# Rounded products first: reordering the products of transposed blocks in an attention kernel

## The chip, the cores and the metric

The kernel runs on one core of one Trainium2 chip, as one launch. The metric is device time in microseconds (us). TensorE is called PE in the rows (its weight loads PEld), VectorE is DVE, ScalarE is ACT, GpSimd is POOL and SyncE, which issues the transfers, is SP.

## The reference

One inference step of a one-layer encoder for two request groups, a prompt of 1024 rows and a sample of 64 rows with a cache of 1024 past rows, with shared weights:

```
shift/scale/gate (x2) = silu(c) @ w_ada + b_ada                      # adaLN, one column set per group
h   = RMSNorm(x) * (1 + scale1) + shift1
u   = h @ w_in                                                       # 1024 -> 3072
mix = concat(differential attention (4 heads), stick-breaking attention (8 heads))
x   = x + gate1 * RMSNorm(mix @ w_out)
x   = x + gate2 * RMSNorm(relu(h2 @ w_up)^2 @ w_down),  h2 as h, with shift2, scale2
```

All data are float32. A differential head applies `softmax(q0 k0) - lam * softmax(q1 k1)` to its values; a stick-breaking head weighs key k by `sigmoid(z_k)` times the product of `1 - sigmoid(z)` over the later keys. Both end in a matrix of weights, queries by keys, times the values.

## The kernel before, in words

**Rounded part and remainder.** Matrix products run in a rounded float32 format. To keep precision, an operand is split: ACT casts it to the rounded format (line 64), and DVE (for some, POOL) subtracts the cast from the original (line 65), which leaves the remainder. A product is then the sum of two or three products into one accumulator. Names that end in h are rounded parts, those that end in l remainders.

**Attention.** Work is cut into units u = 0 to 7: units 0 to 3 are one differential head each, units 4 to 7 are two stick-breaking heads each. A unit has steps: `Diff(u, t)` for 128 query rows, `Stick(u, q, hd)` for 256 query rows of one head, `Sample(u)` for the sample group. A step has a score part (lines 593 and 594 make `pz`; ACT takes exponentials or sigmoids, and a stick-breaking head runs a DVE scan, line 740) and an apply part. The apply part works in groups of up to four 128x128 blocks: PE transposes the blocks into `pt` (line 604), ACT casts `pt` to `ah` (line 64), DVE subtracts to `al` (line 65), and PE multiplies both with the values into `po`. A group is named by its step, as in `ah6_110`: unit 6, q = 1, head 1, blocks 0; `ahS60` is the sample step of unit 6, first cache half.

In `apply_rows` (for Diff and Sample, lines 616 to 623) the blocks are the stationary operand: block by block, a product of 256 columns with `ah` (line 620), then one of 128 columns with `al` (line 621). In `Stick.apply` (lines 781 to 789) the values are stationary and `ah` or `al` streams: for each of two key blocks j, a product with `ah` (line 788), then one with `al` (line 789), 256 columns each, or 128 for the block on the diagonal. `ah` and `al` have two buffers each.

**adaLN's second columns.** `modulation` (line 212) makes shift2 and scale2 in eight pieces during attention: products into `pam` (line 201), a DVE copy to `Rm` (line 224), a small product with `sel` into `pcm` (line 209), then DVE additions.

**What sets the order.** The text interleaves one step's apply with the next step's score (`merge`), and spends a filler between them: projections of the next unit (lines 303 to 305), and from unit 2 on the pieces of `modulation` and `gate_rows`. A generator's `yield c` says how much estimated PE time it has spent; the filler stops at a yield when its debt is paid. On top of this, the program is built with `schedule_with_timeline_sim=True` (line 1302): at build time the framework lays out each engine's list from its own estimate of when each instruction will be ready, and takes first what stands first in the text. So work of other steps stands between neighbours of the text, and a change in the text moves instructions on all engines. On the chip each engine follows its list strictly; a wait stops all that stands behind it there.

**After attention** come the output projection (`py`, lines 1095 to 1098), whose first products are laid between the last attention steps, and the feed-forward part (`pu`, lines 303 to 305; `pd`, lines 1181 to 1184).

Of the kernel before, what the change touches and what calls it, by code (L numbers as in the profile page):

```python
# [16 lines left out]
P = 128  # L17
# [17 lines left out]
def build(tc, I, O):  # L35
# [11 lines left out]
    def big(name, tag, shape, dt=F32R):  # L47
        return sb.tile(shape, dt, tag=tag, name=name, bufs=BUFS[tag])
# [4 lines left out]
    def brief(shape, name, tag, dt=F32, bufs=2):  # L53
        return atp.tile(shape, dt, tag=tag, name=name, bufs=bufs)

    def bank(name, tag):
        return pp.tile([P, 512], F32, tag=tag, name=name)

    load = nc.sync.dma_start
    mm = nc.tensor.matmul  # L60
# [60 lines left out]
    cc = brief([16, P], "cc", "o1", bufs=1)  # L121
# [66 lines left out]
    def ada_rows(c0, name, ps=None, between=()):  # L188


        if ps is None:
            ps = bank("pa" + name, "pj")[:, :256]
        for q in range(2):
            raw = ada_raws.get((c0, q))
            if raw is None:
                raw = big(f"ar{name}{q}", "raw", [P, 4, 256], F32)
                load(raw, w_ada[:, 4 * q : 4 * q + 4, c0 : c0 + 256])
            if q == 1 and between:
                between.pop()()
            for i in range(4):  # L200
                mm(ps[32 * i : 32 * i + 32], lhsT=sc[:, 4 * q + i, :], rhs=raw[:, i, :], start=(q == 0), stop=(q == 1), skip_group_check=True)
            yield 0.5
        return ps

    def sum_to_columns(R, n, name):

        ps = bank(name, "pj")
        for i in range(n):
            mm(ps[:, 2 * i : 2 * i + 2], lhsT=R[:, i * P : (i + 1) * P], rhs=sel, start=True, stop=True)
        return ps[:, 0 : 2 * n].rearrange("p (k j) -> p k j", j=2)  # L210

    def modulation(first, cols, name):

        A, B = (sb.tile([P, KT, 2], F32, name=x + name) for x in "AB")

        def gen():
            for q in range(4):
                ks = slice(2 * q, 2 * q + 2)
                for part in range(2):
                    nm = f"{name}{q}{part}"  # L220
                    c0 = first + D * part + 256 * q
                    ps = yield from ada_rows(c0, nm)
                    R = big("R" + nm, "s", [P, 512], F32)[:, :256]
                    nc.vector.tensor_copy(R, ps)
                    v = sum_to_columns(R, 2, "pc" + nm)
                    col = lambda c: cols[:, c : c + 2].unsqueeze(2).broadcast_to([P, 2, 2])
                    o = (B, A)[part][:, ks, :]
                    nc.vector.tensor_tensor(o, v, col(8 + (c0 - first) // P), ALU.add)
                    if part:
                        nc.vector.scalar_tensor_tensor(o, o, 1.0, col(2 * q), ALU.add, ALU.mult)  # L230
                    yield None

        return A, B, gen()
# [366 lines left out]
    def transposed(srcs, name, kr=P):  # L600

        pt = bank("pt" + name, "tr")
        for i, a in enumerate(srcs):
            nc.tensor.transpose(pt[:kr, i * P : (i + 1) * P], a, ident)  # L604
        n = len(srcs) * P
        ah, al = (small([P, 512], f"{x}{name}", x, F32R, bufs=2) for x in ("ah", "al"))
        split(pt[:kr, :n], ah[:kr, :n], al[:kr, :n])
        return ah, al

    def apply_rows(po, parts, values):  # L610

        n = sum(len(p[0]) for p in parts)
        done = 0
        pend = []

        def times(ah, al, blocks, kr):
            nonlocal done
            for i in range(len(blocks)):
                v = values(done)
                mm(po[:, 0:256], lhsT=ah[:kr, i * P : (i + 1) * P], rhs=v.rearrange("p a d -> p (a d)"), start=(done == 0), stop=False, skip_group_check=True)  # L620
                mm(po[:, 0:P], lhsT=al[:kr, i * P : (i + 1) * P], rhs=v[:, 0, :], start=False, stop=(done == n - 1), skip_group_check=True)
                done += 1

        for blocks, kr, name, pre in parts:
            if pre:
                pre()
            pend.append((*transposed(blocks, name, kr), blocks, kr))
            yield 0.11 * len(blocks)
            if len(pend) == 2:
                times(*pend.pop(0))  # L630
                yield 0.8
        yield 0.1
        while pend:
            times(*pend.pop(0))
            yield 0.8
# [17 lines left out]
    class Diff:  # L653
# [37 lines left out]
        def apply(self):  # L691
            u, t = self.u, self.t
            V = U[u]["V"]
            self.po = po = bank(f"po{self.name}", "pv")
            parts = []
            for c, (c0, w) in enumerate(chunks(P * (t + 1))):
                e0, e1 = self.e[0][c], self.e[1][c]

                def pre(e0=e0, e1=e1):
                    nc.vector.scalar_tensor_tensor(e0, e1, self.cf, e0, ALU.mult, ALU.add)  # L700

                parts.append(([e0[:, i : i + P] for i in range(0, w, P)], P, f"{self.name}{c}", pre))
            yield from apply_rows(po, parts, lambda j: V[:, j])
            le = brief([P, 1], f"le{self.name}", "le", bufs=1)
            nc.gpsimd.tensor_scalar(le, self.l[0], self.l[0], EPS, ALU.mult, ALU.mult)
            od = brief([P, P], f"od{self.name}", "od", bufs=1)
            o1 = brief([P, P], f"o1{self.name}", "o1", bufs=1)
            nc.scalar.copy(o1, po[:, P:256])
            nc.vector.tensor_tensor(od, po[:, 0:P], o1, ALU.add)
            r = rstd(sumsq([od], P, f"ssd{self.name}", [o1]), P, f"rsd{self.name}", add=le, inv=1.0 / P)  # L710
            nc.gpsimd.tensor_scalar(od, od, r, None, ALU.mult)
            self.od = od
# [34 lines left out]
    class Stick:  # L747
# [26 lines left out]
        def apply(self):  # L774
            u, q, hd = self.u, self.q, self.hd
            r, o = slice(64 * hd, 64 * hd + 64), slice(64 - 64 * hd, 128 - 64 * hd)
            V = U[u]["V"]
            po = bank(f"po{self.name}", "pv")
            pend = []

            def times(jp, ah, al):
                for i in range(2):
                    j = 2 * jp + i
                    v = V[:, j, hd, :]
                    lone = j == 2 * q + 1
                    out = po[:, P:256] if lone else po[:, 0:256]
                    cc = slice(256, 384) if lone else slice(256 * i, 256 * i + 256)
                    mm(out, lhsT=v, rhs=ah[:, cc], start=(j == 2 * q), stop=False, skip_group_check=True)  # L788
                    mm(out, lhsT=v, rhs=al[:, cc], start=False, stop=(j == 1), skip_group_check=True)  # L789

            for jp in reversed(range(q + 1)):
                blocks = [(j, t) for j in (2 * jp, 2 * jp + 1) for t in range(2) if not (j == 2 * q + 1 and t == 0)]
                src = [self.w[t][j // 4][:, (j % 4) * P : (j % 4 + 1) * P] for j, t in blocks]
                pend.append((jp, *transposed(src, f"{self.name}{jp}")))
                yield 0.11 * len(src)
                if len(pend) == 2:
                    times(*pend.pop(0))
                    yield 0.43
            yield 0.1
            while pend:  # L800
                times(*pend.pop(0))
                yield 0.43
            if hd == 0:
                mixes[u] = brief([P, 256], f"mx{self.name}", "mx", bufs=1)
            mx = mixes[u]
            ot = brief([P, 256], f"ot{self.name}", "so2", bufs=1)
            nc.scalar.copy(ot[r], po[o, 0:256])
            nc.vector.tensor_tensor(mx[r], po[r, 0:256], ot[r], ALU.add)
            if hd == 1:
                load(mixD[u, :, 256 * q : 256 * q + 256], mx)  # L810
# [421 lines left out]
    for b in range(NB - 1):  # L1232
# [12 lines left out]
        if last:  # L1245
            GG2 = gate("g2", 1, "h")
            wd2 = [down_weights(b + 1, i, i == 0) for i in range(2)]
            done = []
# [57 lines left out]
```

## Time and profile before

| | us |
|---|---|
| three runs | 1546.62, 1553.53, 1556.1 (median 1553.53) |
| profiled execution | 1554.56 |
| its span, first to last instruction | 1552.7 |
| PE busy in the span | 1499.0 (97%), 8714 products and as many weight loads |
| DVE, ACT, POOL busy | 918.1 (59%), 700.1 (45%), 342.7 (22%) |
| mean granted TensorE clock | 0.99 |

Attention lies between about 60 and 690 us of the span, the output projection runs to about 780 us, and the feed-forward part from there to the end. A row of the timeline gives start, duration, engine, line, operation, output<-inputs, and shapes; a bracket at its end is the idle time of the engine ahead of it and what ended it. Starts of PE's products are closer together than their durations, since one product streams in while the one ahead drains; the pace is the distance of the starts. The granted clock is 1.00 at 2.4 GHz and 0.5 at 1.2 GHz.

### The profile page before, as it was taken

The numbers are of one execution on the slowest core, as the hardware profiler recorded it, in microseconds if no ns is written. First come the engines' busy times: TensorE is split into PE (matmuls) and PEld (weight loads), VectorE is DVE, ScalarE is ACT, GpSimd is POOL, SyncE is SP. The second block draws the span as 40 slices with busy tenths as digits, with TensorE's granted clock in tenths as the row PEclk, the third lists the DMA queues.
The fourth block names the chain that finished last, engine by engine and source line by source line (L and its number), as shares of the span: only waits on it lengthen the run. The fifth ranks groups of instructions, "written<-read, shape, count | busy, mean of one in ns | idle before, by whom it ended". The sixth has DMA issues, their size and how long they took to land.

```text
span 1552.7 us, 23586 instructions
## 1 busy us (share of the span) xinstructions
PE 1499.0 (97%) x8714; PEld 1341.8 (86%) x8714; DVE 918.1 (59%) x1761; ACT 700.1 (45%) x1650; POOL 342.7 (22%) x519
## 2 busy tenths in 40 slices
PE   6899999989999999899999999999999999999998
PEld 4789898878899988778898988899989999899896
DVE  3776877675868687866442445454554544544447
ACT  3766766666768577837653112121122112121122
POOL 1453443434333333622110000000000000000002
PEclk9999999999999999999999999999999999999999
DMA  9322333424232325444221122211111111111025
GB/s 315 119 60 82 93 115 100 119 62 124 71 113 60 111 88 159 124 122 140 75 66 52 34 79 82 70 40 41 55 54 41 46 37 42 54 55 41 28 82 183
DMA packets 152517, 133.20 MB, mean 86 GB/s; under 512 B 11234, under 2 KB 136275, under 8 KB 152403
## 3 DMA queue, kind: packets, MB, share of 16 engines
q1 hardware_dynamic: 152402, 131.71, 27.6%
q8 instruction: 68, 1.11, 0.3%
q14 instruction: 47, 0.38, 0.1%
HBM read 108.59 MB, written 23.09 MB: 85 GB/s over the span
## 4 chain that ended last, share of the span: by engine, by line
PE 64%; issue 4%; ACT 4%; DVE 3%; POOL 1%; DMA 1%; SPq 0%; DVEq 0%; POOLq 0%; ACTq 0%
PE pu L303 8%; PE pu L305 8%; PE pu L304 8%; PE pd L1181 8%; PE pd L1182 8%; PE pd L1184 7%; PE py L1096 1%; PE py L1098 1%; PE pt L604 1%; PE py L1095 1%; PE po L789 1%; PE pq L303 1%; PE pq L305 1%; PE pq L304 1%; PE pk L303 1%
## 5 line engine op out<-in xcount | busy, mean ns | idle before, releaser
L1188 DVE TENSOR_TENSOR acc<-pd,acc 128x512 f32<-128x512 f32 x252 | 171.8, 687 | 113.6 <-PE pd L1184 107.8
L1166 ACT ACTIVATE sq<-pu 128x384 f32<-128x384 f32 (+1 forms) x96 | 45.1, 470 | 308.3 <-PE pu L305 308.3
L1167 DVE TENSOR_TENSOR sq<-sq 128x384 f32<-128x384 f32 (+1 forms) x96 | 72.1, 751 | 171.8 <-ACT sq L1166 171.8
L65 DVE TENSOR_TENSOR al<-pt,ah 128x512 fp32r<-128x512 f32 (+2 forms) x128 | 75.6, 598 | 19.1 <-ACT ah L64 17.7
L593 PE MATMUL pz<-K,Q 128*128 128x128 f32 (+2 forms) x192 | 72.9, 382 | 4.5 <-DVE mn L678 1.9
L64 ACT CAST ah<-pt 128x512 fp32r<-128x512 f32 (+2 forms) x128 | 65.9, 522 | 24.5 <-PE pt L604 16.7
L604 PE MATMUL pt<-ident,s 128*128 128x128 f32 x432 | 70.0, 277 | 4.2 <-DVE al L65 1.5
L642 ACT ACTIVATE s<-s,mn 128x512 f32<-128x512 f32 (+3 forms) x96 | 58.6, 611 | 23.3 <-DVE mn L678 19.7
L594 PE MATMUL pz<-Kl,qz 128*128 128x128 f32 (+2 forms) x192 | 66.6, 350 | 0.0
L740 DVE TENSOR_TENSOR_SCAN s<-k,s 128x128 f32<-128x128 f32 (+1 forms) x64 | 58.2, 922 | 11.4 <-POOL s L769 7.1
L604 PEld LDWEIGHTS pt<-ident,s 128*128 128x128 f32 x432 | 51.6, 141 | 9.2 <-DVE al L65 2.0
L65 DVE TENSOR_TENSOR rl<-sq,rh 128x384 fp32r<-128x384 f32 x64 | 35.7, 558 | 38.1 <-ACT rh L64 38.1
L442 POOL CAST qz<-Q 64x256 fp32r<-64x256 f32 x64 | 36.9, 576 | 90.5 <-PE pz L594 71.8
L764 ACT ACTIVATE s<-pz 128x128 f32<-128x128 f32 (+2 forms) x96 | 47.8, 498 | 15.5 <-PE pz L594 14.9
L64 ACT CAST rh<-sq 128x384 fp32r<-128x384 f32 x64 | 32.8, 513 | 40.2 <-DVE sq L1167 38.2
L765 ACT ACTIVATE k<-pz 128x128 f32<-128x128 f32 (+2 forms) x96 | 47.9, 499 | 0.0
L789 PE MATMUL po<-al,V 128*128 128x256 f32 (+1 forms) x160 | 41.4, 293 | 6.3 <-DVE al L65 6.3
L740 DVE TENSOR_TENSOR_SCAN s<-k,s,s 128x512 f32<-128x512 f32 x32 | 43.6, 1371 | 5.1 <-ACT k L765 5.1
L593 PEld LDWEIGHTS pz<-K,Q 128*128 128x128 f32 x192 | 36.6, 191 | 11.2 <-DVE mn L678 4.6
L678 DVE CUSTOM_DVE_ANT_0 s<-pz,T 128x512 f32<-128x512 f32 (+3 forms) x64 | 37.3, 585 | 12.4 <-PE pz L594 11.9
L788 PE MATMUL po<-ah,V 128*128 128x256 f32 (+1 forms) x160 | 43.8, 284 | 0.7 <-ACT ah L64 0.7
L64 ACT CAST r<-sq 128x320 fp32r<-128x320 f32 x32 | 14.8, 461 | 62.7 <-DVE sq L1167 62.7
(1232 smaller groups left out, 5125.5 us busy)
## 6 DMA issues: line engine op xcount, KB each, us to landing
arr<-in_w_ada SPq DMA_DIRECT2D x16, 512.0 KB
arm<-in_w_ada SPq DMA_DIRECT2D x16, 512.0 KB
ar<-in_w_ada SPq DMA_DIRECT2D x10, 512.0 KB
mixD<-mx SPq DMA_DIRECT2D x32, 128.0 KB
xr<-in_x_prompt SPq DMA_DIRECT2D x16, 256.0 KB
xD<-xr SPq DMA_DIRECT2D x16, 256.0 KB
xy<-xD SPq DMA_DIRECT2D x8, 512.0 KB
out_y_prompt<-xy SPq DMA_DIRECT2D x16, 256.0 KB
```

Source lines behind the costliest of these rows:

```text
L64: (eh or nc.scalar.copy)(hi, src)
L65: (el or nc.vector).tensor_tensor(lo, src, fr(hi), ALU.subtract)
L303: mm(ps[:, :n], lhsT=wh[:, k, :], rhs=hh[:, k, :n], start=(k == 0), stop=False)
L304: mm(ps[:, :n], lhsT=wh[:, k, :], rhs=hl[:, k, :n], start=False, stop=False)
L305: mm(ps[:, :n], lhsT=wl[:, k, :], rhs=hh[:, k, :n], start=False, stop=(k == 7))
L593: mm(ps[:, :w], lhsT=S["Q"][m][:, qt], rhs=S["Kd"][m][:, c0 : c0 + w], start=True, stop=False)
L604: nc.tensor.transpose(pt[:kr, i * P : (i + 1) * P], a, ident)
L740: nc.vector.tensor_tensor_scan(d, k, d, 0.0 if later is None else later[:, 0:1], ALU.mult, ALU.add)
L1181: mm(ps, lhsT=rh[:, off : off + P], rhs=wh[:, cols], start=(j == 0), stop=False)
L1182: mm(ps, lhsT=rh[:, off : off + P], rhs=wl[:, cols], start=False, stop=(m == 8 and end))
L1184: mm(ps, lhsT=rl[:, off : off + P], rhs=wh[:, cols], start=False, stop=end)
L1188: nc.vector.tensor_tensor(acc[m][:, cols], ps, acc[m][:, cols], ALU.add)
```

## The change

Three places of the text. In `apply_rows` and in `Stick.apply` the products of a group with the rounded parts come first for all its blocks, then those with the remainders. In `modulation` a yield of 0.2 stands after the copy to `Rm`, so that the filler may stop there and other work may be laid ahead of the product with `sel`. No instruction is added or taken away on any engine.

```diff
@@ modulation
                     R = big("R" + nm, "s", [P, 512], F32)[:, :256]
                     nc.vector.tensor_copy(R, ps)
+                    yield 0.2
                     v = sum_to_columns(R, 2, "pc" + nm)
@@ apply_rows
         def times(ah, al, blocks, kr):
             nonlocal done
-            for i in range(len(blocks)):
-                v = values(done)
-                mm(po[:, 0:256], lhsT=ah[:kr, i * P : (i + 1) * P], rhs=v.rearrange("p a d -> p (a d)"), start=(done == 0), stop=False, skip_group_check=True)
-                mm(po[:, 0:P], lhsT=al[:kr, i * P : (i + 1) * P], rhs=v[:, 0, :], start=False, stop=(done == n - 1), skip_group_check=True)
-                done += 1
+            vs = [values(done + i) for i in range(len(blocks))]
+            for i, v in enumerate(vs):
+                mm(po[:, 0:256], lhsT=ah[:kr, i * P : (i + 1) * P], rhs=v.rearrange("p a d -> p (a d)"), start=(done + i == 0), stop=False, skip_group_check=True)
+            for i, v in enumerate(vs):
+                mm(po[:, 0:P], lhsT=al[:kr, i * P : (i + 1) * P], rhs=v[:, 0, :], start=False, stop=(done + i == n - 1), skip_group_check=True)
+            done += len(blocks)
@@ Stick.apply
             def times(jp, ah, al):
-                for i in range(2):
-                    j = 2 * jp + i
-                    v = V[:, j, hd, :]
-                    lone = j == 2 * q + 1
-                    out = po[:, P:256] if lone else po[:, 0:256]
-                    cc = slice(256, 384) if lone else slice(256 * i, 256 * i + 256)
-                    mm(out, lhsT=v, rhs=ah[:, cc], start=(j == 2 * q), stop=False, skip_group_check=True)
-                    mm(out, lhsT=v, rhs=al[:, cc], start=False, stop=(j == 1), skip_group_check=True)
+                for a in (ah, al):
+                    for j in (2 * jp, 2 * jp + 1):
+                        lone = j == 2 * q + 1
+                        out = po[:, P:256] if lone else po[:, 0:256]
+                        c0 = 256 * (j % 2)
+                        mm(out, lhsT=V[:, j, hd, :], rhs=a[:, c0 : c0 + (P if lone else 256)], start=(a is ah and j == 2 * q),
+                           stop=(a is al and j == 1), skip_group_check=True)
```

What it moves is more than these lines show. Three places follow, each before and then with the change; line numbers grow by one with the change, and by two behind `apply_rows`' first lines.

**On PE, at the end of unit 6's sample step** (`poS6`, with `ahS61` and `alS61` of its second cache half, `ahS60` and `alS60` of its first; `pv72` is a projection for unit 7). Before:

```order
L620 MATMUL poS6_8267<-cv61_8143,ahS61_8291 128x256
L621 MATMUL poS6_8267<-cv61_8143,alS61_8292 128x128
L604 MATMUL pt7_101_8364<-ident_66,s7_1020_8255 128x128
L604 MATMUL pt7_101_8364<-ident_66,s7_1030_8274 128x128 x2
L620 MATMUL poS6_8267<-cv60_8142,ahS60_8316 128x256
L593 MATMUL pz7_2041_8439<-K70_7606,Q70_7501 128x128
L594 MATMUL pz7_2041_8439<-Kl7_7608,qz0_493 128x128
L593 MATMUL pz7_2051_8457<-K70_7606,Q70_7501 128x256
L594 MATMUL pz7_2051_8457<-Kl7_7608,qz0_493 128x256
L621 MATMUL poS6_8267<-cv60_8142,alS60_8317 128x128
```

With the change, where "..." stands for 20 more products into `pv72`:

```order
L621 MATMUL poS6_8284<-cv61_8156,ahS61_8305 128x256 x4
L304 MATMUL pv72_8414<-h1h2_119,wv7h_7496 128x320
L305 MATMUL pv72_8414<-h1l2_120,wv7h_7496 128x320
...
L304 MATMUL pv72_8414<-h1h2_119,wv7h_7496 128x320
L594 MATMUL pz7_2041_8445<-K70_7606,Q70_7501 128x128
L595 MATMUL pz7_2041_8445<-Kl7_7608,qz0_493 128x128
L623 MATMUL poS6_8284<-cv61_8156,alS61_8306 128x128 x4
L621 MATMUL poS6_8284<-cv60_8155,ahS60_8322 128x256 x4
L623 MATMUL poS6_8284<-cv60_8155,alS60_8323 128x128 x4
L605 MATMUL pt7_101_8370<-ident_66,s7_1020_8272 128x128
L605 MATMUL pt7_101_8370<-ident_66,s7_1030_8291 128x128 x2
```

Before, S61's remainder follows each of its rounded products at once, and four score products (`pz7`) stand between the first product with `ahS60` and the first with `alS60`; now 22 projection and two score products stand between S61's four rounded products and its remainders, S60's follow behind, and the transposes of group 7_101 come behind all of it instead of ahead.

**On DVE, over the same stretch** (the scans of line 740 are printed as SCALAR_TENSOR_TENSOR here and write `s7_...`, `ml1` is a remainder for the output projection, `Kl7` one of unit 7's keys). Before:

```order
L65 TENSOR_TENSOR alS61_8292<-ptS61_8286,ahS61_8291 128x512
L740 SCALAR_TENSOR_TENSOR s7_1030_8274<-k7_1030_8275,s7_1030_8274 128x512
L65 TENSOR_TENSOR ml1_9029<-ml1_9029,mh1_9028 128x1152
L489 SCALAR_TENSOR_TENSOR Q71_7502<-pq72_8222,Q71_7502 64x256
L65 TENSOR_TENSOR alS60_8317<-ptS60_8311,ahS60_8316 128x512
L740 SCALAR_TENSOR_TENSOR s7_1120_8351<-k7_1120_8352,s7_1120_8351 128x384
L514 TENSOR_TENSOR Kl7_7608<-pk72_8304,K70_7606 64x256
L740 SCALAR_TENSOR_TENSOR s7_1130_8372<-k7_1130_8373,s7_1130_8372 128x512
L65 TENSOR_TENSOR al7_101_8369<-pt7_101_8364,ah7_101_8368 128x384
```

With the change:

```order
L65 TENSOR_TENSOR alS61_8306<-ptS61_8300,ahS61_8305 128x512
L65 TENSOR_TENSOR alS60_8323<-ptS60_8317,ahS60_8322 128x512
L742 SCALAR_TENSOR_TENSOR s7_1030_8291<-k7_1030_8292,s7_1030_8291 128x512
L742 SCALAR_TENSOR_TENSOR s7_1120_8357<-k7_1120_8358,s7_1120_8357 128x384
L515 TENSOR_TENSOR Kl7_7608<-pk72_8267,K70_7606 64x256
L515 TENSOR_TENSOR Kl7_7608<-pk72_8267,K71_7607 64x256
L742 SCALAR_TENSOR_TENSOR s7_1130_8378<-k7_1130_8379,s7_1130_8378 128x512
L742 SCALAR_TENSOR_TENSOR s7_2041_8443<-k7_2041_8444,s7_2041_8443 128x128
L932 TENSOR_TENSOR sod6_8352<-so26_8351 64x64 x2
L465 COPY ok72_8400<-pnk72_8396 128x256
L468 COPY ok72_8400<-pnk72_8396 64x128
L65 TENSOR_TENSOR al7_101_8375<-pt7_101_8370,ah7_101_8374 128x384
```

The subtraction for S60 moved ahead of the scan `s7_1030`, from four places behind S61's to the next one; the subtraction for 7_101 moved back, behind `Kl7`, a scan and copies.

**On PE, group 6_110 of unit 6** (`pt6_110` are its transposes; `pq70` is a projection). Before, where the first "..." stands for three more products of group 6_111, five transposes, two score products and 15 products into `pq70`, the second for two more into `pq70`, two score products and three transposes:

```order
L604 MATMUL pt6_110_7440<-ident_66,s6_1130_7333 128x128
L593 MATMUL pz6_2141_7524<-K61_6556,Q61_6455 128x128
L594 MATMUL pz6_2141_7524<-Kl6_6557,qz1_494 128x128
L788 MATMUL po6_11_7416<-ah6_111_7421,V6_6667 128x256
...
L788 MATMUL po6_11_7416<-ah6_110_7445,V6_6667 128x256
...
L789 MATMUL po6_11_7416<-al6_110_7446,V6_6667 128x256
L788 MATMUL po6_11_7416<-ah6_110_7445,V6_6667 128x256
L789 MATMUL po6_11_7416<-al6_110_7446,V6_6667 128x256
```

With the change:

```order
L605 MATMUL pt6_110_7434<-ident_66,s6_1130_7327 128x128
L594 MATMUL pz6_2050_7466<-K60_6559,Q60_6468 128x512
...
L789 MATMUL po6_11_7413<-ah6_111_7418,V6_6667 128x256
L789 MATMUL po6_11_7413<-ah6_111_7418,V6_6667 128x128
L789 MATMUL po6_11_7413<-al6_111_7419,V6_6667 128x256
L789 MATMUL po6_11_7413<-al6_111_7419,V6_6667 128x128
...
L605 MATMUL pt6_202_7529<-ident_66,s6_2051_7422 128x128 x2
L594 MATMUL pz6_2141_7521<-K61_6560,Q61_6469 128x128
L595 MATMUL pz6_2141_7521<-Kl6_6561,qz1_494 128x128
L789 MATMUL po6_11_7413<-ah6_110_7439,V6_6667 128x256 x2
...
L789 MATMUL po6_11_7413<-al6_110_7440,V6_6667 128x256 x2
```

Left out here are a score product, a transpose and two transposes of values. The 17 projection products that stood between the transposes of 6_110 and its remainders are gone from there, so its products follow its transposes much sooner. Between the last product into `pam` of the eight pieces of adaLN's columns and the first into `pcm` there stand, piece by piece, 1, 3, 14, 14, 18, 13, 14 and 7 instructions of other steps before, and 8, 7, 17, 15, 25, 13, 17 and 1 with the change. Of the output projection, 19 products of `py11` stand ahead of the product with `alS72` (unit 7's sample step) before, and behind it with the change.

## Rows read from the trace of the kernel before

**Rows 1.** The page, busy time by engine: us, share of the span, instructions.

```profile
PE 1499.0 (97%) x8714; PEld 1341.8 (86%) x8714; DVE 918.1 (59%) x1761; ACT 700.1 (45%) x1650; POOL 342.7 (22%) x519
```

**Rows 2.** Stages: length; busy us by engine; granted clock, DMA share, GB/s.

```profile
80.00:600.00 520.00, 503.68 (x3409) 464.04 (x3408) 375.59 (x882) 354.29 (x942) 200.93 (x320) 1.00 0.31 92
600.00:690.00 90.00, 79.65 (x473) 68.32 (x472) 70.67 (x99) 59.65 (x128) 46.54 (x47) 0.94 0.47 145
780.00:1553.00 773.00, 765.51 (x4022) 688.85 (x4021) 378.91 (x587) 181.84 (x327) 51.98 (x48) 1.00 0.19 59
```

**Rows 3.** PE's waits, 60 to 740 us: total us, times, longest.

```profile
PE po L789 <- DVE al L65: 6.3, 9, 1.1
PE poS L621 <- DVE alS L65: 3.8, 2, 2.2
PE pcm L209 <- DVE Rm L224: 3.1, 4, 1.0
```

**Rows 4.** Timeline of PE: the pace of products with fresh weights.

```profile
245.51 0.33 PE L620 MATMUL po<-V,ah 128*128 128x256 f32 x1
245.68 0.22 PE L621 MATMUL po<-V,al 128*128 128x128 f32 x1
245.74 0.44 PE L594 MATMUL pz<-Kl,qz 128*128 128x512 f32 x1
...
654.99 0.28 PE L867 MATMUL pzS<-Kn,bd 128*128 128x64 f32 x1
655.10 0.28 PE L868 MATMUL pzS<-Kn,bd 128*128 128x64 f32 x1
...
655.87 0.28 PE L789 MATMUL po<-al,V 128*128 128x256 f32 x1
655.99 0.28 PE L788 MATMUL po<-ah,V 128*128 128x256 f32 x1
```

**Rows 5.** Timeline of PE: four of its waits.

```profile
553.26 0.38 PE L789 MATMUL po<-al,V 128*128 128x256 f32 x1 [1.05 <-DVE al L65]
...
609.55 0.61 PE L209 MATMUL pcm<-sel,Rm 128*128 128x2 f32 x4 [1.01 <-DVE Rm L224]
...
624.39 0.48 PE L621 MATMUL poS<-cv,alS 128*128 128x128 f32 x1 [1.57 <-DVE alS L65]
...
675.69 0.47 PE L621 MATMUL poS<-Vn,alS 64*128 64x128 f32 x1 [2.22 <-DVE alS L65]
```

**Rows 6.** Timeline of DVE: three scans and the subtraction for S60.

```profile
618.79 2.96 DVE L740 TENSOR_TENSOR_SCAN s<-k,s 128x512 f32<-128x512 f32 x1
...
623.64 0.69 DVE L65 TENSOR_TENSOR alS<-ptS,ahS 128x512 fp32r<-128x512 f32 x1
...
639.57 1.25 DVE L740 TENSOR_TENSOR_SCAN s<-k,s,s 128x512 f32<-128x512 f32 x1
...
672.14 3.32 DVE L740 TENSOR_TENSOR_SCAN s<-k,s,s 128x512 f32<-128x512 f32 x1
```

**Rows 7.** Timeline of POOL under the last of these scans.

```profile
671.10 3.27 POOL L65 TENSOR_TENSOR wo7l<-wo7r,wo7h 128x1024 fp32r<-128x1024 f32 x1
```

**Rows 8.** Stretches of 10 us at the end of attention, columns as in rows 2.

```profile
620.00:630.00 10.00, 8.06 (x50) 7.66 (x50) 9.86 (x12) 7.02 (x19) 8.12 (x7) 0.83 0.43 143
...
670.00:680.00 10.00, 7.78 (x32) 6.26 (x31) 8.45 (x7) 1.70 (x4) 4.38 (x2) 0.77 0.39 127
680.00:690.00 10.00, 10.00 (x51) 8.39 (x51) 2.38 (x5) 1.54 (x3) 0.00 (x0) 0.89 0.25 68
```

**Rows 9.** Timeline of PE: transposes of groups 6_110 and 7_101 (its last two).

```profile
551.27 0.60 PE L604 MATMUL pt<-ident,s 128*128 128x128 f32 x4
...
621.80 0.44 PE L604 MATMUL pt<-ident,s 128*128 128x128 f32 x2 [0.37 <-DVE s L740]
```

**Rows 10.** Timeline of DVE: the subtractions of the same two groups.

```profile
554.64 0.67 DVE L65 TENSOR_TENSOR al<-pt,ah 128x512 fp32r<-128x512 f32 x1
...
628.60 0.52 DVE L65 TENSOR_TENSOR al<-pt,ah 128x384 fp32r<-128x384 f32 x1
```

## The prediction

> **What bounds the kernel.** I read the page's busy times first, then the stages, then PE's waits, then the timelines of PE, DVE and POOL where these waits lie. PE is busy for 97% of the span [rows 1]: it is the bound, and no other engine comes near. A busy PE need not be at its peak, so the pace matters: products of 256 columns start 0.12 us apart, and a stream of only 64 columns takes 0.11 too [rows 4]. With new weights for every product, nothing goes below about 0.11 in a run. The feed-forward part, 773 us, has 7.5 us in which PE isn't busy, and its lists are nearly untouched [rows 2]; all that the change can reach lies before 690 us. There PE lacks 16.3 us between 80 and 600 us and 10.4 us in the last 90 us of attention, where the clock is also down, at 0.94 [rows 2].
>
> So the change can win only PE's idle time, the clock that goes with it, or a better pace. What ends the idle time is in the waits: 6.3 us in 9 waits for stick-breaking remainders, 3.8 us in 2 for sample remainders, 3.1 us in 4 for the copy ahead of adaLN's columns [rows 3], 13.2 us together. These are exactly the waits that the change aims at. With them come two falls of the clock to its lower level, 1.2 of 2.4 GHz: after the wait of 1.57 us at 624 us the stretch's mean is 0.83, after that of 2.22 us at 675 us it is 0.77 and 0.89 [rows 5, 8]. At full load a stretch loses its missing share: 0.17 x 10 = 1.7 us, and (0.23 + 0.11) x 10 = 3.4 us.
>
> **The work itself: 0.** No instruction is added or removed, and each product still loads its own weights (as many loads as products [rows 1]). In Diff and Sample a pair of 256 and 128 columns takes 0.17 + 0.06 = 0.23 us today [rows 4]. A group of four is 0.92. Regrouped it is four of 0.12 and four short ones; the nearest row to a run of short ones is the run of 64 columns, 0.11, so 0.48 + 0.44 = 0.92 again. Bounds: if a short one kept its 0.06 in a run, each of some 200 pairs would win 0.05, 10 us in all; if a rounded one kept 0.17, each would lose 0.05, 10 us, which the 0.12 of two neighbouring products excludes. I take 0, since the 64-column run shows that a short stream alone doesn't buy a faster pace. The Trainium skill, "TensorE: Matmul & The Clock Gate", section "Back-to-back issue gap", gives about 81 ns for a product of 128 columns in a sustained stream with weight loads; by that the term would be an estimated 200 x 0.03 = 6 us of gain. The 0.11 of an even shorter product here speaks against it.
>
> **The direct effect on the waits: -1.4 us.** If all else stood still, a remainder's product would start later by the rounded products now ahead of it: one more, 0.12 us, in a stick-breaking group of two key blocks, three more, 0.35, in S60, none in the sample group of one block (the wait at 675 us). 9 x 0.12 + 0.35 = 1.4. That is small against waits of 1 to 2 us. They are long because DVE is late: the scan ahead of the last one takes 3.32 us where the same shape took 1.25, under a POOL subtraction that runs from 671.10 to 674.37 [rows 6, 7]. The Trainium skill, "GPSIMD Engine Reference", section "Specifications", says that POOL shares its interfaces to SBUF with VectorE, with contention for DVE instructions of two SBUF inputs; the rows agree. It speaks against this change, which leaves both instructions where they are.
>
> **What the new order does beyond that: -2.6 us.** The framework lays out the lists anew from its own estimate of readiness. It can lay other work into the slack, or pull a group closer and spend the slack again. Both happen, as the pieces of the lists show.
>
> - S60 (first and second place): its subtraction is now ahead of the scan that took 2.96 us [rows 6], and 22 products of mostly 320 columns, 0.14 us each at 2.4 GHz and 3 us together, stand ahead of S61's remainders. The wait of 1.57 us [rows 5] should go, and with it the fall at 624 us: -1.6 beyond the 0.35 already counted is -1.2, the clock -1.7.
> - Groups 6_100 and 6_111: their waits, one of them 1.05 us [rows 5], go, since a score and projections moved between: -1.0.
> - adaLN's columns: for six of eight pieces more work of other steps stands ahead of the product; for the last it is one instruction where it was seven. Of the four waits, 3.1 us [rows 3], the three earlier ones, 2.1, lose 1.5; the last, 1.01 us [rows 5], grows by six products of 0.11 to 0.16, +0.8. Bounds -3.1 (all go) and +0.8 (none of the others does).
> - Group 7_101: its transposes now come behind S60. Before, 7.3 us went by from its last transposes to its remainder (621.80 to 629.12 [rows 9, 10]), behind scans that are still ahead of it on DVE. The work now between is 3 transposes, 4 transposes, two products of 256, two of 320, two of 512 columns and two of its own: 2.0 us. Part of its delay passes while PE does S60, so I take +2; bounds 0 and 7.3 - 2.0 = 5.3.
>
> Sum: -1.2 - 1.7 - 1.0 - 1.5 + 0.8 + 2.0 = -2.6; with the direct effect -4.0 us. The wait at 675 us stays, and so does its fall: with the change the same subtraction has one long scan ahead of it instead of two, but all 19 output products that stood ahead of its product on PE stand behind it now, so PE is there some 4 us sooner. What hides the moved projections is that PE would do them anyway; they cost nothing as long as no later group waits for want of them.
>
> **The number.** The profiled execution took 1554.56 us (span 1552.7 us and 1.9 us around it), 1.0 above the median of the three runs, 1553.53. 1554.6 - 4.0 = 1550.6; beside the median 1549.5. I say 1550.
>
> **Rivals.**
> 1. The waits go altogether: 13.2 us, and both falls, 5.1 us, -18.3: 1536 us. For it: these are the waits the new order is made for, at 553, 609 and 624 us. Against: the DVE work that makes them late isn't touched, and the layout uses up slack.
> 2. Slower, by groups that now come too soon. Five groups (4_000, 5_110, 6_110, 7_100, 7_101) had over 5 us of PE work between their transposes and their first remainder product and have 1.8 to 2.2 us now (counted from the lists: 0.11 us for each transpose and short product, otherwise columns at 2.4 GHz). The third place shows one. 6_110 took 551.27 to 555.31, less 0.33 for its four transposes, 3.7 us to its remainder [rows 9, 10]; against 2.0 it would miss 1.7. Four such are 6.8, 7_101 at its bound 5.3, a fall of the clock behind that 1.7: +13.8, 1568 us. It decides if ACT and DVE are as late for these groups as before; since their lists moved along with PE's, I expect them mostly in time. If the gains above come too, it is 1562.
> 3. Runs of short products do go faster than the 64-column row says, the bound of 10 us: 1540 to 1544 us. For it: the pair's 0.06; against: that 0.06 is paid back by the 0.17 ahead of it. The skill's section named above stands for this case and gives an estimated 1544.
>
> That the products aren't regrouped is excluded by the lists; that the yield lays no work ahead holds for two of eight pieces.
>
> **Chances.** Forecast 0.57, on its own 1543 to 1558; rival 1 0.20, rival 2 0.17, rival 3 0.06. A difference under 1% (15.5 us) is no change for a measurement of this kernel, whose three runs differ by 9.5 us. Under 1538 us lie some six tenths of rival 1 and a little of the forecast and rival 3, 0.18; over 1569 us half of rival 2 and a little of the forecast, 0.11; the rest, 0.71, is no change. The range takes rival 1 and rival 2 at their numbers: 1536 to 1566.
>
> **What would show it.** In the profile after: waits of PE for remainders at 6 us or less instead of 10.1; no wait of over 0.5 us at S60 and no fall near 624 us; waits for the copy ahead of adaLN's columns near 2.4 us, mostly at the last piece; four short products in a run at 0.11. Wrong if PE's idle time between 80 and 690 us is under 12 us (rival 1) or over 36 us (rival 2), or if a run of short products starts every 0.06 us (rival 3).

## The result, and the profile after

The changed kernel took 1561.74 us (median of six runs, 1558.63 to 1563.13), the kernel before 1552.86 (six runs, 1546.62 to 1556.10). The ratio is 1.0059, 95% interval 1.0041 to 1.0078: 9 us slower, where I had forecast 3.5 us faster. The profiled execution took 1562.46 us, its span is 1559.3 us.

The page after, busy us by engine; it answers to [rows 1]:

```profile
PE 1504.8 (97%) x8714; PEld 1344.7 (86%) x8714; DVE 923.2 (59%) x1761; ACT 700.7 (45%) x1650; POOL 333.3 (21%) x519
```

The stages after, columns as in [rows 2] (the last stretch now ends at the same 1553 us, 6 us ahead of the end):

```profile
80.00:600.00 520.00, 504.44 (x3370) 461.94 (x3370) 375.27 (x873) 349.45 (x930) 195.02 (x318) 0.99 0.31 92
600.00:690.00 90.00, 77.40 (x479) 67.04 (x478) 76.23 (x105) 63.57 (x138) 43.61 (x49) 0.96 0.44 138
780.00:1553.00 773.00, 771.92 (x4060) 694.78 (x4058) 381.91 (x592) 186.14 (x335) 53.48 (x46) 1.00 0.19 59
```

PE's idle time from 80 to 690 us is 15.6 + 12.6 = 28.2 us, against 26.7 before [rows 2]. That is only 1.5 us more. The rest shows in the output projection. Its products in the window from 630 us to attention's last product, first of the kernel before, then of the changed one (PE busy and count come first):

```profile
630.00:699.10 69.10, 31.96 (x120) 22.67 (x121) 2.58 (x4) 0.69 (x2) 0.95 0.40 122
```

```profile
630.00:699.80 69.80, 26.07 (x95) 17.61 (x96) 1.29 (x2) 0.98 (x3) 0.95 0.40 121
```

Attention's last product starts at the same time, 699 to 700 us (the "about 690" ahead of the prediction was too early), but 25 products fewer of the output projection are done by then. They have to follow, 0.23 us each, 5.8 us. The first product of the feed-forward part starts at 773.98 us before and at 780.57 after, and from there on nothing changes:

```profile
773.98 0.34 PE L303 MATMUL pu<-h2h,wu00h 128*128 128x384 f32 x1
```

```profile
780.57 0.34 PE L304 MATMUL pu<-h2h,wu00h 128*128 128x384 f32 x1
```

So PE lost 6.6 us before 780 us. PE's waits after (60 to 740 us: total, times, longest), which answer to [rows 3]:

```profile
PE po L789 <- DVE al L65: 9.8, 7, 3.0
PE po L789 <- ACT ah L64: 2.5, 3, 1.9
PE po L621 <- DVE od L711: 1.5, 1, 1.5
...
PE pcm L209 <- DVE Rm L224: 0.5, 1, 0.5
```

No product into `poS` waits for a sample remainder any more, and adaLN's columns wait 0.5 us instead of 3.1. But stick-breaking remainders cost 9.8 us instead of 6.3, and rounded parts (`ah`) 2.5 instead of 0.7. The timeline has other places than [rows 5]:

```profile
298.20 0.38 PE L621 MATMUL po<-V,ah 128*128 128x256 f32 x1 [1.12 <-ACT mx L651]
...
345.81 0.62 PE L621 MATMUL po<-V,ah 128*128 128x256 f32 x3 [1.50 <-DVE od L711]
...
479.79 0.39 PE L789 MATMUL po<-al,V 128*128 128x256 f32 x1 [1.72 <-DVE al L65]
...
590.32 0.39 PE L789 MATMUL po<-ah,V 128*128 128x256 f32 x1 [1.85 <-ACT ah L64]
...
615.20 0.50 PE L209 MATMUL pcm<-sel,Rm 128*128 128x2 f32 x3 [0.51 <-DVE Rm L224]
...
639.35 0.45 PE L789 MATMUL po<-al,V 128*128 128x256 f32 x2 [2.07 <-DVE al L65]
...
675.45 0.58 PE L789 MATMUL po<-al,V 128*128 128x256 f32 x1 [3.02 <-DVE al L65]
```

The first two belong to differential units and wait for ACT's `mx` and DVE's `od` (a difference of two heads), the one at 615 us is adaLN's, and the other four are groups 5_111, 6_300, 7_101 and 7_301. The clock falls five times instead of twice [rows 8]:

```profile
295.00:305.00 10.00, 8.33 (x44) 6.92 (x44) 6.52 (x24) 5.18 (x18) 2.04 (x5) 0.83 0.22 67
345.00:355.00 10.00, 9.19 (x63) 7.59 (x64) 7.17 (x21) 4.93 (x18) 3.94 (x7) 0.83 0.56 171
475.00:485.00 10.00, 8.02 (x46) 7.10 (x45) 8.13 (x14) 7.67 (x18) 4.89 (x6) 0.83 0.44 133
640.00:650.00 10.00, 9.12 (x49) 7.63 (x48) 9.82 (x12) 7.75 (x20) 5.43 (x8) 0.83 0.66 202
670.00:680.00 10.00, 6.98 (x33) 5.84 (x31) 9.18 (x10) 4.35 (x9) 4.99 (x5) 0.83 0.53 163
```

Each misses 0.17 x 10 = 1.7 us of full clock, 8.5 together; before it was 5.1. With the 1.5 us of idle time that is 4.9 of the 6.6 us.

Why is a remainder late? The timeline of DVE ahead of group 7_301, and of ACT (the cast that the subtraction needs), both after:

```profile
667.30 2.25 DVE L732 TENSOR_TENSOR sst<-sst,skt 128x63 f32<-128x63 f32 x1
669.47 3.43 DVE L731 TENSOR_TENSOR_SCAN sk<-sk,skt 128x512 f32<-128x512 f32 x1
672.93 0.69 DVE L732 TENSOR_TENSOR ss<-ss,sk 128x511 f32<-128x511 f32 x1
673.54 1.27 DVE L731 TENSOR_TENSOR_SCAN sk<-sk,sk 128x511 f32<-128x511 f32 x1
674.73 0.66 DVE L65 TENSOR_TENSOR al<-pt,ah 128x512 fp32r<-128x512 f32 x1
```

```profile
669.05 0.62 ACT L64 CAST ah<-pt 128x512 fp32r<-128x512 f32 x1
```

The cast ended at 669.67, the subtraction began at 674.73. For 5.1 us everything it needs is there, and DVE is busy with what stands ahead of it in its list. For 6_300 the same happens on ACT, where the cast stands behind one for the output projection that waits for a transfer:

```profile
588.63 1.15 ACT L64 CAST mh<-ml 128x1152 fp32r<-128x1152 f32 x1 [0.38 <-DMA ml<-mixD]
589.69 0.58 ACT L64 CAST ah<-pt 128x512 fp32r<-128x512 f32 x1
```

### The profile page after: what moved, and what is told of

It reads as the page before. It is cut to its first block, busy times and chain, and to the rows that moved or that the text cites. A ratio compares the mean times of both kernels' runs of the same rounds, so it can differ in the third digit from the quotient of the medians.

```text
span 1559.3 us, 23585 instructions
## 1 busy us (share of the span) xinstructions
PE 1504.8 (97%) x8714; PEld 1344.7 (86%) x8714; DVE 923.2 (59%) x1761; ACT 700.7 (45%) x1650; POOL 333.3 (21%) x519
## 4 chain that ended last, share of the span: by engine, by line
PE 79%; DVE 5%; ACT 4%; issue 4%; DMA 2%; POOL 1%; SPq 0%; DVEq 0%; POOLq 0%; ACTq 0%
PE pu L304 8%; PE pu L306 8%; PE pu L305 8%; PE pd L1182 8%; PE pd L1183 8%; PE pd L1185 7%; PE pt L605 2%; PE pq L304 2%; PE pq L305 2%; PE pk L304 2%; PE pk L306 2%; PE pq L306 2%; PE pk L305 2%; PE pz L594 2%; PE po L789 2%
## 5 line engine op out<-in xcount | busy, mean ns | idle before, releaser
L742 DVE TENSOR_TENSOR_SCAN s<-k,s,s 128x512 f32<-128x512 f32 x32 | 47.2, 1486 | 8.5 <-ACT k L767 8.4
L443 POOL CAST qz<-Q 64x256 fp32r<-64x256 f32 x64 | 31.7, 496 | 85.7 <-PE pz L595 72.4
L789 PE MATMUL po<-al,V 128*128 128x256 f32 (+1 forms) x160 | 33.9, 294 | 10.0 <-DVE al L65 9.8
L771 POOL TENSOR_SCALAR_AFFINE_SELECT s<-s 128x128 f32<-128x128 f32 x64 | 26.3, 415 | 76.5 <-ACT s L766 59.3
```

The costliest lines, as they stand in the source:

```text
L742: nc.vector.tensor_tensor_scan(d, k, d, 0.0 if later is None else later[:, 0:1], ALU.mult, ALU.add)
```

## The experiments

The experiments are told by argument; "second", "fifth" and the like count them in the order in which they ran, and each place names its number. They ran in four sets (1 to 4, 5 to 8, 9 to 12, 13), each beside runs of the kernel before, whose median was 1551.67 to 1553.04 us. Within a set medians are compared, across sets the ratios to the kernel before.

**Text or layout** (first to third). The change does two things: it alters the order within groups, and it makes the framework lay out all lists anew. To part them I fixed a layout: behind the program's text, each engine's instructions are chained in the order of a given list, by edges that only set the order of issue. With before's own text this gives before's lists, instruction for instruction; with the regrouped text each group's products take the same places on PE, rounded parts first (four pairs of neighbours on DVE stand the other way round). In the profile of the ninth experiment, which has before's text and a fixed layout, PE's list is that of before throughout. In the code, `seq` is one engine's instructions in the order of the list:

```diff
+def freeze(tc, nc, skip=()):
...
+        for a, b in zip(seq, seq[1:]):
+            tc.add_manual_dep(b, a.name, mybir.DependencyInfo(mybir.DependencyClass.NoSync, mybir.DependencyReason.DATA), reason="layout")
...
         build(tc, I, O)
+        freeze(tc, nc)
```

The first experiment has both regroupings without the yield, and the framework lays it out itself:

```diff
-                    yield 0.2
```

> Both regroupings without the yield in modulation; the framework lays the lists out anew, and 896 products stand elsewhere than before (1161 with the whole change). Theory A (the loss comes from the new layout that the regrouped text leads to): slower than before by most of the 9 us, 1558 to 1563 us. Theory B (the order of the products within a group itself costs): 1562 us as well. Theory C (the yield, which shifts what the filler has paid, is the cause): as before, 1553 us.

Measured: 1559.48 us against 1551.67 before, ratio 1.0045 (1.0031 to 1.0060).

The second has the same text in before's layout:

> The regrouped text of both places, but every engine's list is fixed to the layout of the kernel before: each group's products take the same places on PE as before, only their order within these places is rounded parts first. Nothing else moves on any engine. Theory A: the direct effect alone, -1.4 us by the prediction, so 1551 to 1553 us. Theory B: 1562 us. Rival 3 of the prediction (runs of short products go faster) would show here as 1543 us.

Measured: 1549.90 us, 0.9987 (0.9970 to 1.0003). Of the waits in [rows 3], the two for remainders are shorter, 8.4 us together instead of 10.1:

```profile
PE po L788 <- DVE al L65: 5.2, 8, 1.1
PE poS L622 <- DVE alS L65: 3.2, 2, 2.0
```

The third has before's text in the layout of the first (five pairs of neighbours on DVE exchanged):

> The text of before (block by block, rounded part then remainder), but every engine's list is fixed to the layout that both regroupings led to (that of the first kernel of this set). Theory A: as slow as that kernel or up to 2 us slower, 1560 to 1564 us. Theory B: as before, 1553 us.

Measured: 1572.16 us, 1.0127 (1.0102 to 1.0153), slower than expected.

| us | layout of before | new layout |
|---|---|---|
| block by block | 1551.7 | 1572.2 |
| rounded parts first | 1549.9 | 1559.5 |

The layout costs 9.6 us with the regrouped text and 20.5 with the old one. The regrouping gains in both, 1.8 us (an interval of -4.7 to +0.5) and 12.7. Theory B falls: in neither layout does the regrouping cost time. Of the two, A is left, though it had given the third experiment no more than 1564 us. The new layout suits the order that it was made for: with products block by block the first remainder comes ahead of the second rounded part, and PE waits more for stick-breaking remainders, though less for those of the samples. First the new layout with regrouped products, then with the old order:

```profile
PE po L788 <- DVE al L65: 7.7, 10, 1.7
PE poS L622 <- DVE alS L65: 7.2, 3, 5.8
```

```profile
PE po L789 <- DVE al L65: 17.9, 14, 3.5
...
PE poS L621 <- DVE alS L65: 2.1, 3, 1.1
```

**The yield alone** (fourth).

```diff
                     nc.vector.tensor_copy(R, ps)
+                    yield 0.2
                     v = sum_to_columns(R, 2, "pc" + nm)
```

> Only the yield of 0.2 in modulation; the lists are laid out anew, 444 products stand elsewhere. Theory A: some change of either sign, since the layout is another one; by the 6 output-projection products fewer ahead of attention's last product (25 fewer with the whole change, for 9 us) about +2, 1555 us. Theory B: 1553 us. Theory C: 1562 us.

Measured: 1565.06 us, 1.0086 (1.0057 to 1.0115). The size is theory C's, but the yield isn't the only cause, since the first experiment is slow without it. The parts don't add: 7.8 and 13.4 alone, 8.9 together. My estimate by the count of output-projection products fell: 6 fewer, 13 us.

**Two numbers that have nothing to do with the change** (seventh and eighth).

```diff
-                yield 0.11 * len(src)
+                yield 0.12 * len(src)
```

> The text of before with one number changed that has nothing to do with the change: the yield behind a stick-breaking group's transposes counts 0.12 us per block instead of 0.11, so the filler spends a little more there; 480 products stand elsewhere. Theory A in its wide form (the layout of before is a favourable one among many, and nearly any other is slower): slower by 3 to 14 us, 1555 to 1566 us. Its narrow form (only where the text's order in the groups or in modulation changes is the layout worse): 1550 to 1553 us.

Measured: 1556.61 us against 1552.70 before, 1.0031 (1.0011 to 1.0051).

```diff
-    cost = [st.cost for st in steps]
+    cost = [st.cost * (1.02 if isinstance(st, Sample) else 1) for st in steps]
```

> The text of before with another such number changed: the cost that the planner counts for a sample step, 2% more. 869 products stand elsewhere, and 21 fewer output-projection products stand ahead of attention's last product. Theory A, wide: 1555 to 1566 us. Narrow: 1550 to 1553 us.

Measured: 1558.05 us, 1.0041 (1.0022 to 1.0061). With the change, its part without the yield and the yield alone, five new layouts are slower by 4 to 13 us, and none is faster. That is theory A in its wide form, as far as five layouts show it.

**Where in the layout** (eleventh and twelfth). Two layouts were joined at 600 us, with the regrouped text.

> The regrouped text; up to 600 us the layout of before, behind that the layout of the first experiment (both regroupings, no yield). The second and first experiment, 1549.9 and 1559.5 us, are its two ends. By the idle time and low clock in their profiles the new layout loses some 2.6 us up to 600 us and 6.8 behind it: here 1556 to 1558 us if the tail is the place (theory: where output-projection products should fill PE and DVE is loaded), 1552 to 1553 if the loss lies earlier.

Measured: 1555.40 us against 1553.04, 1.0013 (0.9999 to 1.0027).

> The other way round: the regrouped text, up to 600 us the layout of the first experiment, behind that the layout of before. 1552 to 1553 us if the tail is the place of the loss, 1556 to 1558 if it lies earlier.

Measured: 1557.38 us, 1.0022 (1.0010 to 1.0035). By the ratios, the new layout behind 600 us costs 0.0026, 4.0 us, against the layout of before throughout (0.9987), and the new layout up to 600 us costs 0.0035, 5.4 us. Together that is 9.4, as much as the whole layout costs, 9.0 by its ratio. I had expected 6.8 behind 600 us and 2.6 ahead of it; the tail isn't the one place.

**DVE's queue** (fifth, ninth, tenth, sixth and thirteenth). If the subtractions are late only by their place in DVE's list, moving them there must help, with nothing moved on PE. The moves were written into the fixed lists, shown here by names in place of the program's numbers:

```diff
 # DVE's list (before's layout, regrouped text), one of eight moves
-  scan s7_3171, scan s7_3160, al: alS72
+  al: alS72, scan s7_3171, scan s7_3160
```

> The regrouped text in the layout of before (as in the second experiment), and eight subtractions on DVE moved ahead of the scans or of the output projection's subtractions that stood in front of them (al5_111, al6_111, alS60, al7_202, al7_200, al7_212, al7_211, alS72). In the profile of the second experiment their inputs had been ready 1.2 to 7.2 us before DVE came to them, and PE waited for them 0.3 to 2.2 us, 8.3 us in all. Theory D (these waits are DVE's queue, not PE's order, and the layout puts the subtractions too late because it counts on shorter scans): the waits go, with them the clock fall behind the one at 650 us, 1.7 us: 1540 to 1544 us. Rival: the scans that are now later make PE wait as long for their transposes, or the moved work shows up at the output projection: 1549 to 1551 us.

Measured: 1545.07 us against 1552.70, 0.9948 (0.9931 to 0.9965): 7.6 below the kernel before and, by the ratios, 6.1 below the second experiment (4.8 by the medians), so it beats both kernels. It is 1 us short of the expected 1540 to 1544. Of its waits for stick-breaking remainders 1.3 us are left, and PE is busier at the end of attention than in [rows 2]:

```profile
PE po L788 <- DVE al L65: 1.3, 4, 0.5
```

```profile
600.00:690.00 90.00, 82.45 (x489) 70.36 (x488) 68.05 (x98) 59.29 (x127) 46.44 (x46) 0.96 0.50 154
```

That the layout puts the subtractions late because it counts on shorter scans, as the expectation says, no run shows.

The ninth experiment has the same eight moves with the products block by block:

> The kernel before, text and layout, with only the eight subtractions of the fifth experiment moved ahead on DVE; the products stay block by block. Theory D: the gain of that move doesn't need the regrouping; -5 to -8 us, 1545 to 1548 us. Rival (the moved subtractions only pay with the remainders' products last): 1550 to 1553 us.

Measured: 1546.36 us against 1553.04, 0.9958 (0.9944 to 0.9972). The gain doesn't need the regrouping.

The tenth makes four more moves:

> As the fifth experiment (regrouped, layout of before, eight subtractions ahead), and four more moves on DVE: three copies to Rm (Rm211, Rm230, Rm231) ahead of the scan that stands in front of them, and a subtraction for the cached keys (ckl7) ahead of two others. In the fifth's profile PE waited 0.8, 1.0, 1.1 and 1.6 us there, and 6.8 us of low clock, 3.4 us lost, begin at the last one. Theory D: -4 to -8 against it, 1537 to 1541 us. Rival (the scans now come late, or PE meets the next thing that is missing, since PE's waits are set by the whole chain): 1543 to 1546 us.

Measured: 1546.82 us, 0.9965 (0.9952 to 0.9979): nothing gained, and 0.8 us above the range of the rival, which names the reason as far as one is known. In the profile, of an execution of 1551.04 us, other waits have grown. That they are for instructions which the moved ones had pushed, or which PE now reached sooner, is argued and not shown:

```profile
PE po L788 <- DVE al L65: 3.7, 6, 1.2
...
PE poS L622 <- DVE alS L65: 1.8, 1, 1.8
```

The sixth is the changed kernel in its own layout, with seven moves of this kind:

> The changed kernel with its own layout on every engine, but seven subtractions on DVE moved ahead of the scans in front of them (al5_111, al7_101, al7_202, al7_201, al7_212, al7_211, al7_301). In its profile their inputs had been ready 1.1 to 5.1 us before DVE came to them, and PE waited 0.3 to 3.2 us for them, 10.8 us in all; three of its clock falls (480, 641, 675 us) stand right behind such waits, 1.7 us each. Theory D: most of the 10.8 and of the 5.1 come back, 1548 to 1552 us, about as fast as before. Rival (the loss lies elsewhere in the layout: the falls at 300 and 347 us, the early stretch, the pace): 1557 to 1562 us.

Measured: 1556.15 us against 1552.70, 1.0023 (1.0006 to 1.0041). 5.6 of the 9 us are back, between the two expectations. The thirteenth makes five moves more, one of them on ACT:

> The changed kernel in its own layout, with the seven subtractions of the sixth experiment moved ahead on DVE and five more instructions, which its profile shows ready 0.7 us or more before their engine came to them, with PE waiting: a difference of two heads (od3_4, PE waited 1.5 us), a query split (Q71, 1.5 us), a copy for the mix (mx7_10, 1.2 us) and al7_111 on DVE, and on ACT the cast ah6_300, which stood behind a cast for the output projection that waited for a transfer (2.1 us). Theory D (the new layout's loss is a number of single places where an engine's list puts a late or long instruction ahead of what PE wants): 6.3 us of waits and the two low-clock spells behind them, 345 and 588 us, 1.7 us each: 1548 to 1552 us, as fast as before. Rival (what remains is spread too thin, or comes back elsewhere, as in the tenth experiment): 1554 to 1557 us.

Measured: 1554.71 us against 1552.88, 1.0004 (0.9988 to 1.0019). That lies in the rival's range. The step itself, 1.4 us by the medians and 2.9 by the ratios, is far smaller than the 6.3 us and more that theory D gave; but twelve moved instructions, none on PE, have brought the changed kernel to where no difference from before can be measured. Of its profile, the stages:

```profile
80.00:600.00 520.00, 506.95 (x3394) 465.15 (x3394) 374.38 (x877) 351.06 (x936) 197.29 (x320) 0.99 0.31 92
600.00:690.00 90.00, 80.22 (x489) 67.22 (x488) 75.98 (x108) 62.68 (x137) 46.11 (x48) 0.98 0.49 152
```

PE is idle for 13.1 + 9.8 = 22.9 us there, 5.3 less than with the change alone and 3.8 less than before. The profiled execution, 1555.82 us, is no faster than that of before all the same, with as many falls of the clock; where the rest goes isn't traced.

These moves don't explain what parts the two layouts. They gain about as much in the layout of before (6.1 us in the fifth experiment, 6.7 in the ninth) as in the changed kernel's (5.6 in the sixth). The fifth and sixth, of one set and with eight and seven moves, are 11.1 us apart; without moves the second experiment (0.9987) and the changed kernel (1.0059) are 11.2 us apart by the ratios. Late subtractions are a cost of either layout.

## Why the prediction was wrong, step by step

**The work itself, 0: right.** Four short products in a run take 0.40 us and four of 256 columns ahead of them 0.52, 0.92 together as forecast. The timeline of PE after, which answers to [rows 4]:

```profile
142.68 0.69 PE L621 MATMUL po<-V,ah 128*128 128x256 f32 x4
143.20 0.56 PE L623 MATMUL po<-V,al 128*128 128x128 f32 x4
143.60 0.44 PE L869 MATMUL pzS<-ckl,bd 128*128 128x512 f32 x1
```

Rival 3, 10 us, is excluded by this and by the second experiment, whose interval ends at -4.7 us; so is the estimate of 6 us beside it.

**The direct effect, -1.4 us: fits.** The second experiment is that step by itself, -1.8, though its interval reaches over zero. The waits agree: 1.1 us less for stick-breaking remainders, as 9 x 0.12 gives, and 0.6 less for those of the samples, of which S60 has the 0.35 of the sum (1.22 us instead of 1.57).

**"What the new order does beyond that: -2.6 us": failed.** The runs put +9.6 us in its place without the yield (first against second experiment), and +10.7 with it (8.9 for the whole change and 1.8 for the direct effect). Its terms were mostly right where I looked. The wait at S60 and its clock fall are gone; in that step S61's first product waits 0.71 us for its cast. Groups 6_100 and 6_111 wait no more for remainders. adaLN's columns win 2.6 us instead of 0.7. 7_101 waits 2.07 us, +2 as said, though not for the fall of the clock behind it. The wait for S72 at 675 us, which I kept, is gone too, with 7_301 in its place; in the first experiment's layout it is there, at 5.8 us. What failed is that I took the places I had looked at for the whole. The lists are redrawn everywhere, and places that I had put at nothing came up: 1.12 and 1.50 us at 298 and 346 us, 1.72 for 5_111 (0.92 before), 1.85 for 6_300 and 3.02 for 7_301, with four of the five falls of the clock, 6.8 us.

**The measure was wrong as well.** For rival 2, which had the right sign, I took the time from a group's transposes to its remainder from the trace of before, and set it against the work on PE in between. Of its five groups, 7_101 waited noticeably for its remainder, and the waits of 5_111, 7_301 and 6_300 stood outside it. For that time isn't a property of the group. It is what happens to stand ahead on DVE or ACT, and how long that takes, 5.1 us for 7_301. I had the clue in hand: the scan of 3.32 us ahead of S72's subtraction under a POOL subtraction [rows 6, 7]. I used it for that place only. After, `sk` takes 3.43 us at 669.47, and 1.27 at 673.54. Over the first of them, and over the stretched `sst` ahead of it, POOL runs subtractions for the output projection:

```profile
667.02 2.44 POOL L65 TENSOR_TENSOR wo4l<-wo4r,wo4h 128x1024 fp32r<-128x1024 f32 x1
669.42 2.40 POOL L65 TENSOR_TENSOR wo5l<-wo5r,wo5h 128x1024 fp32r<-128x1024 f32 x1
```

The rule of the Trainium skill that the prediction names ("GPSIMD Engine Reference", section "Specifications"), contention of POOL with DVE instructions of two SBUF inputs, agrees with these rows too; no run here took the POOL work away.

**The signs that I named.** Waits for remainders came to 9.8 us instead of 6 or less: wrong. No wait and no fall at S60, and 0.5 us for adaLN's columns: right, the latter better than said. PE's idle time, 28.2 us, lies between the marks of rivals 1 and 2, and the kernel is slower all the same: the marks left out the clock, which lost 3.4 us more.

**The rival that was missing** is the layout as a whole: a constant of the text that changes nothing in the work costs 4 to 5 us here, by the two experiments with such numbers. What stays open is why this layout is better than the five others. That the numbers in its text were chosen by its times, and so favour it, is an argument and not shown. 1.7 of the 6.6 us before the feed-forward part are not traced to a row either.

## What to carry to other kernels

Where a framework lays out the lists, a change of the text is two changes: fix the layout, measure the edit in it, and price the new layout by itself, with unrelated edits as its yardstick. Where an engine waits for another, look first at when the awaited instruction's inputs were ready: if long before, its place in its own engine's list is the cause, and moving it there paid more here (6.1 us) than reordering the engine that waits (1.8). Such moves stopped paying after the worst few. And a repair that gains as much in the kernel before doesn't show what the change lost: try it in both.

## What the hardware showed

Whether a scan is slow hangs on which started first, it or the POOL subtraction. In the profile of before, five scans of 128x512 that started behind a subtraction of 128x1024 ended 1.08 or 1.09 us after it; five such subtractions that started behind a scan ended 2.15 to 2.21 us after the scan. That is as if the later one did its whole work only then. First before, where the scan starts 0.39 us behind the subtraction; then the fifth experiment, where the first of two scans starts 0.14 us ahead, and the subtraction takes 4.44 us instead of the 2.40 of `wo5l` above:

```profile
668.79 3.43 DVE L740 TENSOR_TENSOR_SCAN s<-k,s 128x512 f32<-128x512 f32 x1
```

```profile
668.40 2.74 POOL L65 TENSOR_TENSOR wo6l<-wo6r,wo6h 128x1024 fp32r<-128x1024 f32 x1 [2.29 <-PE pz L593]
```

```profile
665.85 1.21 DVE L741 TENSOR_TENSOR_SCAN s<-k,s 128x512 f32<-128x512 f32 x1
666.99 1.25 DVE L741 TENSOR_TENSOR_SCAN s<-k,s,s 128x512 f32<-128x512 f32 x1
```

```profile
665.99 4.44 POOL L65 TENSOR_TENSOR wo6l<-wo6r,wo6h 128x1024 fp32r<-128x1024 f32 x1 [2.21 <-PE pz L593]
```

So the order on DVE sets how long a scan takes, too: before, the second of this pair took 3.32 us [rows 6].

A small DVE instruction can be stretched as much as a scan: `sst`, 128x63, took 2.25 us at 667.30 under POOL's `wo4l` (shown above), and 0.22 us at another place of the profile of the fifth experiment:

```profile
604.34 0.22 DVE L731 TENSOR_TENSOR sst<-sst,skt 128x63 f32<-128x63 f32 x1
```

Not each long wait is followed by a fall of the clock. Behind the wait of 1.85 us at 590.32 (as behind one of 1.68 at 656.93) the changed kernel's clock stayed at its upper level:

```profile
588.00:598.00 10.00, 8.15 (x56) 8.02 (x55) 7.40 (x13) 5.58 (x15) 1.90 (x4) 1.00 0.37 115
```

The runs of a kernel differ in it as well: over the runs of the first four experiments the mean granted clock was 0.992 for the kernel before, 0.990 for the first, 0.991 for the second and 0.986 for the third and fourth. For a PE that is busy nearly throughout some 1550 us, the difference of 0.006 is an estimated 9 us, about half of what the third and two thirds of what the fourth lose.
